# A decoder layer on one core: where the feed-forward weights are prepared, and a norm that is called two up steps later

## The chip, the cores and the metric

The kernel runs on one core of a Trainium2 chip. The metric is the device time of one execution in microseconds (us). The core has a matrix engine (TensorE, PE in the rows; PEld is its weight load), VectorE (DVE), ScalarE (ACT), GpSimd (POOL), and SyncE (SP), whose queue starts the DMA transfers. Each engine works through its own instructions in a fixed order.

## The reference, cut to what matters

One layer of a hybrid decoder over a prompt of 2048 tokens and a sample group of 32 tokens. The change lies at its end:

```
x  = x + concat(ya, yb, yc, yd) @ w_out            # (tokens, 1024)
hn = rmsnorm(x, norm_ffn_g)
x  = x + square(relu(hn @ w_up)) @ w_down          # 1024 -> 4096 -> 1024
y  = rmsnorm(x, norm_final_g)
```

## The kernel before, in words

All matrix products are done with pairs of 16-bit halves: a float32 operand is scaled and split into a high half (a copy on ScalarE) and a low half (a subtraction on VectorE, `split`, L176 and L177), and three products stand for one. The products of the feed-forward stage are also arranged as a fast 2x2 block scheme with seven products instead of eight, so operands are first added and subtracted in blocks (`combine` for the activations, four GpSimd passes for the weights, L2036 to L2039 and L2062 to L2065).

**Blocks and chunks.** The prompt is cut into four blocks of 512 tokens, each two pairs of 128-token tiles. The feed-forward stage holds two blocks at a time: first blocks 2 and 3 (`s` = 0), then 0 and 1 (`s` = 1). Block 2 also carries the sample's tokens: its hn has 136 columns a pair, 272 together, where the others have 256. The 4096 hidden columns are cut into 16 chunks `c` of 256. A step is (s, c, b): `up` makes seven product groups of 12 matmuls (tiles px and pb), squares and splits them into the tile ht; `down` adds 14 groups of three matmuls of 512 columns into x on VectorE (L2191), and for block 2 first the sample's product from the small tile hs (L2128, L2129) into a pd bank, added to accs (L2166). The loop at the end of `ffn` names up of step n+1, then one preparation, then down of step n.

**Preparation.** `ffn_wu` loads 1 MB of w_up into a staging buffer (ws, tag "sw", two buffers), scales and splits it into wu (two buffers). `ffn_wd` does so for w_down into wd and wdT (tag "w", four buffers, at first held by the weights of w_out). In the first pair of blocks the scale is found as well (`wscale`: a square on ScalarE, one small matmul into a pd bank, a power on GpSimd, four small VectorE steps).

**Before the stage.** `outproj` does the w_out products of blocks 0 and 1, then of block 2, then (L1940) of block 3, each product 48 matmuls into a px bank. After block 2's products come `ffn_wu(0, 0)`, block 2's `norm_pair` twice, and `out_sample`, which loads the sample's input x_s, adds its own w_out product and makes its part of hn. `norm_pair` works tile by tile: square (L1959), root (L150, L151), normalised rows xn (L1962), eight transposes (L144) in two PSUM banks, copied to xt (L1967); then tt by subtractions (L1973 to L1976) and the halves of hn (L1980, L1981).

**Buffers.** Tiles with one tag share a ring of buffers. Tag "xn" (two): the norm's xn, x_s, os and every ht. Tag "cat" (two): the inputs of a w_out product, xt and tt of block 3's norm, and the tile fr of every up. Tag "sw" (two): ws, and xt and tt of the other norms. PSUM: px two banks, pb five, pd one. Inside `ffn` the tag "t", which the transposes use, means pd; in `outproj` at that point it means pb.

**Order.** Instructions are named in the order of the program, which is their priority; a list scheduler then fixes each engine's order at build time, taking the ready instruction that was named first.

Of the kernel before, what the change touches and what calls it, by code (L numbers as in the profile page):

```python
# [10 lines left out]
F16 = mybir.dt.float16  # L11
BF = mybir.dt.bfloat16
I32 = mybir.dt.int32
AF = mybir.ActivationFunctionType
OP = mybir.AluOpType
# [8 lines left out]
NS = 32  # L24
# [3 lines left out]
BLOCKS = [(2, 3), (0, 1)]  # L28
# [75 lines left out]
class K:  # L104
# [1772 lines left out]
    def outproj(self, ctx, mix):  # L1877

        nc, A = self.nc, self.A
# [29 lines left out]
        for b in BLOCKS[1]:  # L1909
            for i in range(2):  # L1910
# [4 lines left out]
                hn = rot.tile([128, 7, 4, 2, 128], F16, name="hnr")  # L1915
# [3 lines left out]
        first = [load(2 * BLOCKS[0][0] + i, BLOCKS[0][0], i) for i in range(2)]  # L1919
# [8 lines left out]
        self.accs = self.hp.tile([128, 8, NS], F32, name="accs")  # L1928
        self.wsc = self.hp.tile([128, 2, 4096 // FC, 2], F32, name="wsc")
        self.x2, self.hn = {}, {}  # L1930
        for b in BLOCKS[0]:
            n = 128 + (NS // 4 if b == BLOCKS[0][0] else 0)
            hn = self.hp.tile([128, 2, 7, 4, 2, n], F16, name=f"hn{b}", tag=f"hn{b}")
            prs = first
            if b != BLOCKS[0][0]:
                prs = [load(2 * b + i, b, i) for i in range(2)]

                for i, t, m in ((i, t, m) for m in (0, 2) for i in range(2) for t in range(2)):
                    product(*prs[i], t, m)
            if b == BLOCKS[0][0]:  # L1940
                self.ffn_wu(0, 0)
            for i in range(2):
                self.norm_pair(prs[i][1], gb, hn[:, i, :, :, :, 0:128], b == BLOCKS[0][1])
            if b == BLOCKS[0][0]:
                self.out_sample(hn, g8)
            self.x2[b] = [x2 for _, x2 in prs]
            self.hn[b] = hn

# [121 lines left out]
    def ffn(self):  # L2070
        nc, A, O = self.nc, self.A, self.O
# [2 lines left out]
        nc.sync.dma_start(gf, dram(A["norm_final_g"], 0, [[0, 128], [1, D]]))  # L2074
        accs = self.accs
        NC_ = 4096 // FC
        self.ffn_wd(0, 0)

        def up(s, c, b):

# [40 lines left out]
                nc.scalar.activation(x, x, AF.Square)  # L2121
            hs = None
            if n > 128:
                hs = self.hp.tile([128, 2, 2, 2, 2, 8], F16, name="hs", bufs=2)
                for m in range(2):
                    for t in range(2):
                        x = C[:, ((0, 2), (3, 1))[m][t], :].rearrange("p (i n) -> p i n", i=2)[:, :, 128:]
                        nc.scalar.activation(hs[:, m, 0, t], x, AF.Copy)  # L2128
                        nc.vector.tensor_sub(hs[:, m, 1, t], x, hs[:, m, 0, t])  # L2129


            ht = self.fp.tile([128, 7, 2, N], F16, name="ht", tag="xn", bufs=2)
# [20 lines left out]
        def down(s, c, b, ht, f):  # L2153
            ht, hs = ht
            n = ht.shape[3] // 2
            wd = self.wts[s, c][2]
            if hs is not None:
                p = self.ps("o", [128, 8, 2, NS])
                for m in range(8):
                    for k in range(2):  # L2160

                        x, o = hs[:, k].rearrange("p a t i n -> p (a t i n)"), p[:, m].rearrange("p a n -> p (a n)")
                        self.mm(o, wd[:, k, 0, m * 128:(m + 1) * 128], x, start=m + k == 0, stop=False)
                        self.mm(o[:, 0:NS], wd[:, k, 1, m * 128:(m + 1) * 128], x[:, 0:NS], start=False, stop=k == 1)
                for a in range(2):
                    nc.vector.scalar_tensor_tensor(accs, p[:, :, a, :], f, accs, op0=OP.mult, op1=OP.add)  # L2166
                if c == NC_ - 1:
                    self.ffn_sample_out(gf)
            for i in range(2):
                if (s, c) in PLAIN:  # L2170
                    down_plain(wd, self.x2[b][i], ht[:, :, :, i * n:i * n + 128], f)
                else:
                    down_pair(wd, self.wts[s, c][3], self.x2[b][i], ht[:, :, :, i * n:i * n + 128], f)
                if c == NC_ - 1:
                    for t in range(2):
                        tok = (4 * b + 2 * i + t) * 128
                        self.final(self.x2[b][i][:, t, :], 128, gf, O["y_prompt"][0, tok:tok + 128, :],
                                   (b, i) != (BLOCKS[1][1], 1))
# [39 lines left out]
                    nc.vector.scalar_tensor_tensor(o, p, f, o, op0=OP.mult, op1=OP.add)  # L2218


        steps = [(s, c, b) for s in range(2) for c in range(NC_) for b in BLOCKS[s]]
        first = BLOCKS[0][0]
        ht, f = up(*steps[0]), None
        for n, (s, c, b) in enumerate(steps):
            if b == BLOCKS[s][0]:

                _, iu, _, _, idn = self.wts[s, c]
                f = self.col("ff", bufs=4)
                nc.vector.tensor_scalar(f, iu, self.ish, 1.0 / RS, op0=OP.mult, op1=OP.mult)
                nc.vector.tensor_mul(f, f, f)  # L2230
                nc.vector.tensor_mul(f, f, idn)
            nx = up(*steps[n + 1]) if n + 1 < len(steps) else None
            if (s, c) != (1, NC_ - 1):
                (self.ffn_wu if b == BLOCKS[s][0] else self.ffn_wd)(s + (c + 1) // NC_, (c + 1) % NC_)
            down(s, c, b, ht, f)
            if s == 0 and c == NC_ - 1:
                self.ffn_load(b, BLOCKS[1][BLOCKS[0].index(b)])
            ht = nx
# [66 lines left out]
```

## Time and profile before

| | |
|---|---|
| median of 3 runs | 2594.4 us (2593.81 to 2594.45) |
| profiled execution | 2598.28 us, span 2596.5 us, mean granted TensorE clock 0.972 |
| busy share | TensorE 94%, VectorE 77%, ScalarE 51%, GpSimd 47% |
| chain that ended last | TensorE 51%, VectorE 16%, GpSimd 13%, DMA 6%, ScalarE 6% |

The span runs from the first to the last instruction of the profiled execution. The feed-forward stage begins near 1293 us and takes the rest. In a timeline a row is a start, a length, the engine, the line in the kernel, the operation with output and input, a count, and in brackets how long the engine stood idle before it and what ended that. The length of a row with several instructions runs to the end of the last.

### The profile page before, as it was taken

How to read it: one execution, taken by the hardware profiler on the slowest of the kernel's cores; microseconds unless marked ns; L12 is line 12 of the kernel's file. 1: busy time of each engine (PE TensorE's matmuls, PEld its weight loads, DVE VectorE, ACT ScalarE, POOL GpSimd, SP SyncE). 2: the span in 40 equal slices, each digit the busy share in tenths (PEclk: the TensorE clock that was granted, in tenths of full speed). 3: DMA queues.
4: the chain of work that ended last, by engine and by line, in shares of the span. 5: the costliest groups of instructions: out<-in, count | busy, mean ns of one | idle time of the engine just before them, and what ended most of it. 6: DMA issues, size and time to landing. Idle time of an engine off the chain costs nothing.

```text
span 2596.5 us, 51309 instructions
## 1 busy us (share of the span) xinstructions
PE 2439.7 (94%) x20496; PEld 1663.5 (64%) x20496; DVE 2010.8 (77%) x3746; ACT 1313.2 (51%) x2449; POOL 1212.3 (47%) x1265
## 2 busy tenths in 40 slices
PE   7989999999999899999979999999998999999997
PEld 6975554454467677689856666666665666666664
DVE  7566667874576777654589998889997898999996
ACT  6534332033346677562455555665556454555554
POOL 3403122223114566550255555656556665666652
PEclk9989999999999998999979999999999999999999
DMA  6333416879632433356111111111135211121201
GB/s 176 102 81 86 99 30 218 302 248 334 224 101 77 136 96 104 101 171 216 52 41 50 51 64 50 49 66 34 62 124 214 74 62 49 53 66 49 66 33 65
DMA packets 209321, 277.78 MB, mean 107 GB/s; under 512 B 42837, under 2 KB 177106, under 8 KB 198810
## 3 DMA queue, kind: packets, MB, share of 16 engines
q1 hardware_dynamic: 195050, 202.65, 25.0%
q0 software_dynamic: 9376, 67.64, 7.2%
q10 hardware_dynamic: 4656, 4.23, 0.5%
q8 instruction: 160, 2.62, 0.4%
q14 instruction: 79, 0.65, 0.1%
HBM read 217.33 MB, written 54.29 MB: 105 GB/s over the span
## 4 chain that ended last, share of the span: by engine, by line
PE 51%; DVE 16%; POOL 13%; DMA 6%; ACT 6%; issue 5%; SPq 1%; POOLq 0%; DVEq 0%; ACTq 0%
PE pb L140 25%; PE px L140 23%; DVE x L2191 4%; DVE wu L177 2%; PE pd L140 2%; DMA kp<-in_cache_v_dram,ptV 1%; DVE wd L177 1%; PE pb L144 1%; POOL ht L2146 1%; POOL ws L2037 1%; POOL ht L2148 1%; DVE wdT L177 1%; POOL ws L2039 1%; POOL ws L2038 1%; POOL ws L2036 1%
## 5 line engine op out<-in xcount | busy, mean ns | idle before, releaser
L140 PEld LDWEIGHTS <-wu 128*128 128x128 f16 x5376 | 530.3, 99 | 222.9 <-issue 37.3
L2191 DVE SCALAR_TENSOR_TENSOR x<-pb,ff,x 128x512 f32<-128x512 f32 x840 | 591.3, 740 | 27.3 <-PE pb L140 23.3
L140 PE MATMUL px<-hn,wu 128*128 128x256 f16 (+1 forms) x3072 | 428.0, 276 | 14.6 <-DVE hn L1981 7.0
L140 PEld LDWEIGHTS <-ht 128*128 128x128 f16 x2712 | 264.5, 99 | 231.6 <-issue 26.0
L140 PE MATMUL pb<-wdT,ht 128*128 128x512 f16 x1440 | 379.8, 381 | 15.8 <-DVE x L2191 9.2
L140 PE MATMUL px<-xT,w 128*128 128x512 f16 (+1 forms) x1968 | 371.9, 341 | 1.5 <-ACT da L731 1.2
L140 PE MATMUL pb<-wd,ht 128*128 128x512 f16 x1272 | 336.8, 381 | 6.1 <-DVE x L2191 5.2
L140 PE MATMUL pb<-hn,wu 128*128 128x256 f16 (+1 forms) x2304 | 303.6, 277 | 15.8 <-DVE x L2191 7.6
L140 PEld LDWEIGHTS <-w 128*128 128x128 f16 x2160 | 168.6, 99 | 188.1 <-issue 30.9
L909 POOL TENSOR_TENSOR pl<-P,ph 128x512 f16<-128x512 f32 (+3 forms) x160 | 166.9, 1053 | 155.5 <-ACT ph L906 59.6
L176 ACT ACTIVATE wu<-ws,wsc 128x1024 f16<-128x1024 f32 (+1 forms) x128 | 129.4, 1036 | 130.8 <-POOL ws L2039 76.7
L140 PE MATMUL px<-w,cat 128*128 128x256 f16 x1536 | 180.2, 274 | 3.4 <-DMA cat<-cat 3.3
L177 DVE SCALAR_TENSOR_TENSOR wu<-ws,wsc,wu 128x1024 f16<-128x1024 f32 (+1 forms) x128 | 168.6, 1331 | 18.0 <-ACT wu L176 17.7
L140 PEld LDWEIGHTS <-cat 128*128 128x128 f16 x1536 | 149.6, 98 | 25.7 <-DMA cat<-cat 3.4
L140 PE MATMUL px<-w,xT 128*128 128x128 f16 (+1 forms) x2400 | 156.1, 225 | 10.2 <-DVE v L576 4.5
L140 PEld LDWEIGHTS <-xT 128*128 128x128 f16 (+1 forms) x2672 | 153.1, 101 | 15.5 <-issue 5.5
L902 ACT ACTIVATE P<-pb,nck,cc 128x512 f32<-128x512 f32 (+3 forms) x160 | 112.2, 710 | 75.4 <-PE pb L140 69.7
L2143 ACT ACTIVATE ht<-fr 128x1024 f16<-128x1024 f32 (+1 forms) x60 | 64.2, 1070 | 159.9 <-POOL fr L2149 159.9
L2146 POOL TENSOR_TENSOR ht<-fr,ht 128x512 f16<-128x512 f32 (+1 forms) x60 | 84.2, 1403 | 113.0 <-ACT ht L2145 113.0
L2062 POOL TENSOR_TENSOR ws<-ws 128x512 f32<-128x512 f32 x30 | 41.1, 1371 | 187.1 <-DVE wd L177 187.1
L871 DVE TENSOR_REDUCE mx<-pb 128x1 f32<-128x512 f32 (+3 forms) x160 | 94.8, 607 | 40.0 <-PE pb L140 38.9
L2120 ACT ACTIVATE fr<-fr 128x256 f32<-128x256 f32 (+1 forms) x192 | 77.0, 414 | 90.5 <-DVE fr L2101 89.7
(717 smaller groups left out, 4647.1 us busy)
## 6 DMA issues: line engine op xcount, KB each, us to landing
ws<-in_w_up_dram SPq DMA_DIRECT2D x32, 1024.0 KB
ws<-in_w_down_dram SPq DMA_DIRECT2D x32, 1024.0 KB
ws<-in_w_in_dram SPq DMA_DIRECT2D x22, 512.0 KB
x<-in_x_prompt_dram SPq DMA_DIRECT2D x16, 512.0 KB
cat<-cat SPq DMA_DIRECT2D x32, 256.0 KB
x<-in_x_prompt_dram SPq DMA_DIRECT2D x8, 1024.0 KB
out_y_prompt_dram<-x SPq DMA_DIRECT2D x32, 256.0 KB
hnD<-hnr SPq DMA_DIRECT2D x4, 1792.0 KB
```

Of the source, the lines that this page charges most:

```text
L140: self.nc.tensor.matmul(out, lhsT, rhs, start=start, stop=stop, skip_group_check=True)
L144: self.nc.tensor.transpose(out, in_, self.ident[:n, :n])
L176: self.nc.scalar.activation(hi, x, AF.Copy, scale=sc)
L177: self.nc.vector.scalar_tensor_tensor(lo, x, sc, hi, op0=OP.mult, op1=OP.subtract)
L871: nc.vector.tensor_reduce(mx[:, ii, jb:jb + 1], s[:, :n], axis=AX.X, op=OP.max)
L902: nc.scalar.activation(P[:, :n], s[:, :n], AF.Exp, bias=nck[:, j, h, kt:kt + 1], scale=cc[:, h // 2:h // 2 + 1])
L909: (nc.gpsimd if 1 else nc.vector).tensor_sub(pl[:, :n], P[:, :n], ph[:, :n])
L2062: nc.gpsimd.tensor_sub(B11, B12, B11)
L2120: nc.scalar.activation(x, x, AF.Relu)
L2143: nc.scalar.activation(ht[:, o:o + m, 0, :], x, AF.Copy)
L2146: nc.gpsimd.tensor_sub(ht[:, 0:2, 1, :], C[:, 0:2, :], ht[:, 0:2, 0, :])
L2191: nc.vector.scalar_tensor_tensor(o, p, f, o, op0=OP.mult, op1=OP.add)
```

## The change

`ffn_wu` of chunks 0 and 1 are both named before block 2's norm. `ffn_wd` of chunk 0 is named in the middle of block 3's products. Block 3's norm is kept as two calls in `self.late`, made in the loop of `ffn` after two ups. The steps start with block 2 in chunks 0 and 1, then block 3 in chunks 0 and 1; the later ones alternate as before. After each down one preparation is named: w_down of the next chunk after an even step, w_up of the chunk after that after an odd one. The factor f is kept for each chunk. hs gets another layout and is made by two ScalarE copies and two VectorE subtractions a chunk instead of four each; the sample's matmuls read it with a stride.

```diff
--- before.py
+++ after.py
@@ -1928,6 +1928,8 @@
         self.accs = self.hp.tile([128, 8, NS], F32, name="accs")
         self.wsc = self.hp.tile([128, 2, 4096 // FC, 2], F32, name="wsc")
         self.x2, self.hn = {}, {}
+        self.ffn_wu(0, 0)
+        self.ffn_wu(0, 1)
         for b in BLOCKS[0]:
             n = 128 + (NS // 4 if b == BLOCKS[0][0] else 0)
             hn = self.hp.tile([128, 2, 7, 4, 2, n], F16, name=f"hn{b}", tag=f"hn{b}")
@@ -1936,13 +1938,17 @@
                 prs = [load(2 * b + i, b, i) for i in range(2)]
 
                 for i, t, m in ((i, t, m) for m in (0, 2) for i in range(2) for t in range(2)):
+                    if (i, t, m) == (0, 0, 2):
+                        self.ffn_wd(0, 0)
                     product(*prs[i], t, m)
+            norms = [lambda x=prs[i][1], h=hn[:, i, :, :, :, 0:128], last=b == BLOCKS[0][1]: self.norm_pair(x, gb, h, last)
+                     for i in range(2)]
             if b == BLOCKS[0][0]:
-                self.ffn_wu(0, 0)
-            for i in range(2):
-                self.norm_pair(prs[i][1], gb, hn[:, i, :, :, :, 0:128], b == BLOCKS[0][1])
-            if b == BLOCKS[0][0]:
+                for norm in norms:
+                    norm()
                 self.out_sample(hn, g8)
+            else:
+                self.late = norms
             self.x2[b] = [x2 for _, x2 in prs]
             self.hn[b] = hn
 
@@ -2074,7 +2080,6 @@
         nc.sync.dma_start(gf, dram(A["norm_final_g"], 0, [[0, 128], [1, D]]))
         accs = self.accs
         NC_ = 4096 // FC
-        self.ffn_wd(0, 0)
 
         def up(s, c, b):
 
@@ -2121,12 +2126,13 @@
                 nc.scalar.activation(x, x, AF.Square)
             hs = None
             if n > 128:
-                hs = self.hp.tile([128, 2, 2, 2, 2, 8], F16, name="hs", bufs=2)
-                for m in range(2):
-                    for t in range(2):
-                        x = C[:, ((0, 2), (3, 1))[m][t], :].rearrange("p (i n) -> p i n", i=2)[:, :, 128:]
-                        nc.scalar.activation(hs[:, m, 0, t], x, AF.Copy)
-                        nc.vector.tensor_sub(hs[:, m, 1, t], x, hs[:, m, 0, t])
+
+                hs = self.hp.tile([128, 2, 4, 2, 8], F16, name="hs", bufs=2)
+                for q in range(2):
+                    x = C[:, 2 * q:2 * q + 2, :].rearrange("p o (i n) -> p o i n", i=2)[:, :, :, 128:]
+                    d = [hs[:, a, q:4 - q:3 - 2 * q] for a in range(2)]
+                    nc.scalar.activation(d[0], x, AF.Copy)
+                    nc.vector.tensor_sub(d[1], x, d[0])
 
 
             ht = self.fp.tile([128, 7, 2, N], F16, name="ht", tag="xn", bufs=2)
@@ -2159,9 +2165,9 @@
                 for m in range(8):
                     for k in range(2):
 
-                        x, o = hs[:, k].rearrange("p a t i n -> p (a t i n)"), p[:, m].rearrange("p a n -> p (a n)")
+                        x, o = hs[:, :, 2 * k:2 * k + 2].rearrange("p a t i n -> p a (t i n)"), p[:, m]
                         self.mm(o, wd[:, k, 0, m * 128:(m + 1) * 128], x, start=m + k == 0, stop=False)
-                        self.mm(o[:, 0:NS], wd[:, k, 1, m * 128:(m + 1) * 128], x[:, 0:NS], start=False, stop=k == 1)
+                        self.mm(o[:, 0], wd[:, k, 1, m * 128:(m + 1) * 128], x[:, 0], start=False, stop=k == 1)
                 for a in range(2):
                     nc.vector.scalar_tensor_tensor(accs, p[:, :, a, :], f, accs, op0=OP.mult, op1=OP.add)
                 if c == NC_ - 1:
@@ -2218,21 +2224,28 @@
                     nc.vector.scalar_tensor_tensor(o, p, f, o, op0=OP.mult, op1=OP.add)
 
 
+
         steps = [(s, c, b) for s in range(2) for c in range(NC_) for b in BLOCKS[s]]
-        first = BLOCKS[0][0]
-        ht, f = up(*steps[0]), None
+        steps[1], steps[2] = steps[2], steps[1]
+
+        chunks = [(s, c) for s in range(2) for c in range(NC_)]
+        prep = [p for n in range(1, len(chunks))
+                for p in [(self.ffn_wd, chunks[n])] + [(self.ffn_wu, c) for c in chunks[n + 1:n + 2]]]
+        ht, f = up(*steps[0]), {}
         for n, (s, c, b) in enumerate(steps):
-            if b == BLOCKS[s][0]:
+            if (s, c) not in f:
 
                 _, iu, _, _, idn = self.wts[s, c]
-                f = self.col("ff", bufs=4)
-                nc.vector.tensor_scalar(f, iu, self.ish, 1.0 / RS, op0=OP.mult, op1=OP.mult)
-                nc.vector.tensor_mul(f, f, f)
-                nc.vector.tensor_mul(f, f, idn)
+                f[s, c] = g = self.col("ff", bufs=4)
+                nc.vector.tensor_scalar(g, iu, self.ish, 1.0 / RS, op0=OP.mult, op1=OP.mult)
+                nc.vector.tensor_mul(g, g, g)
+                nc.vector.tensor_mul(g, g, idn)
             nx = up(*steps[n + 1]) if n + 1 < len(steps) else None
-            if (s, c) != (1, NC_ - 1):
-                (self.ffn_wu if b == BLOCKS[s][0] else self.ffn_wd)(s + (c + 1) // NC_, (c + 1) % NC_)
-            down(s, c, b, ht, f)
+            while self.late:
+                self.late.pop(0)()
+            down(s, c, b, ht, f[s, c])
+            if n < len(prep):
+                prep[n][0](*prep[n][1])
             if s == 0 and c == NC_ - 1:
                 self.ffn_load(b, BLOCKS[1][BLOCKS[0].index(b)])
             ht = nx
```

## Rows read from the trace of the kernel before

**Rows 1.** Page, first part: busy us (share of the span) x instructions.

```profile
PE 2439.7 (94%) x20496; PEld 1663.5 (64%) x20496; DVE 2010.8 (77%) x3746; ACT 1313.2 (51%) x2449; POOL 1212.3 (47%) x1265
```

**Rows 2.** Windows: length, busy of PE, PEld, DVE, ACT, POOL, granted clock, DMA.

```profile
1293.00:1333.00 40.00, 22.21 (x137) 17.00 (x136) 35.90 (x37) 25.01 (x34) 23.05 (x16) 0.66 0.13 46
1333.00:1357.00 24.00, 22.35 (x179) 15.51 (x178) 13.54 (x29) 16.18 (x33) 11.18 (x14) 0.93 0.10 35
1357.00:1900.00 543.00, 521.09 (x3868) 348.78 (x3866) 492.84 (x789) 315.09 (x562) 317.72 (x295) 1.00 0.16 53
1900.00:2060.00 160.00, 148.15 (x1032) 98.08 (x1031) 138.43 (x196) 91.52 (x177) 103.98 (x99) 0.96 0.43 153
2060.00:2520.00 460.00, 454.53 (x3106) 304.52 (x3104) 426.88 (x564) 234.72 (x432) 288.62 (x247) 0.99 0.17 56
...
1943.00:1948.00 5.00, 4.88 (x28) 3.57 (x28) 4.32 (x8) 0.80 (x2) 0.00 (x0) 0.55 0.90 330
```

**Rows 3.** Timeline of PE: start us, length us, work [idle before <- releaser].

```profile
1257.62 35.23 PE L140 MATMUL px<-w,cat 128*128 128x256 f16 x319
1292.68 1.91 PE L144 MATMUL pb<-cst,xn 128*128 128x128 f32 x16
...
1294.57 1.55 PE L140 MATMUL px<-hn,wu 128*128 128x272 f16 x12
...
1303.39 1.97 PE L144 MATMUL pb<-cst,xn 128*128 128x128 f32 x8 [4.21 <-DVE wsc L191]
1305.15 4.94 PE L140 MATMUL pb<-hn,wu 128*128 128x272 f16 x24
...
1353.84 2.75 PE L140 MATMUL pb<-wdT,ht 128*128 128x512 f16 x12
...
1943.12 4.91 PE L140 MATMUL pb<-hn,wu 128*128 128x256 f16 x24 [4.45 <-DVE x L2191]
```

**Rows 4.** Timelines of ACT, then DVE: the norm's steps.

```profile
1206.38 0.60 ACT L1967 ACTIVATE xt<-pd 128x512 f32<-128x512 f32 x1 [2.68 <-PE pd L144]
...
1211.75 1.04 ACT L1959 ACTIVATE xn<-x 128x1024 f32<-128x1024 f32 x1
...
1280.11 1.04 ACT L1959 ACTIVATE xn<-x 128x1024 f32<-128x1024 f32 x1
...
1277.34 0.48 DVE L1981 TENSOR_TENSOR hn<-os,hn 128x128 f16<-128x128 f32 x2
...
1282.17 1.28 DVE L1962 SCALAR_TENSOR_TENSOR xn<-x,n_rstd,gb 128x1024 f32<-128x1024 f32 x1 [3.56 <-POOL n_rstd L151]
```

**Rows 5.** Timeline of SP's queue.

```profile
1246.17 0.35 SPq L1987 DMA_DIRECT2D x_s<-in_x_sample_dram  x1
```

**Rows 6.** Timelines of DVE, then POOL: preparation of chunk 0, the sample's chain.

```profile
1241.58 0.15 DVE L191 TENSOR_SCALAR wsc<-w_m 128x1 f32<-128x1 f32 x1
...
1259.05 0.69 DVE L1973 TENSOR_TENSOR tt<-xt 128x512 f32<-128x512 f32 x1
...
1260.52 5.82 POOL L2007 TENSOR_TENSOR os_rs<-os_rs,mhalf 128x32 f32<-128x32 f32 x1 [4.01 <-DVE os_rs L2006]
```

**Rows 7.** Groups: page, then DVE 1330 to 1960, then ACT 1500 to 2500.

```profile
L2062 POOL TENSOR_TENSOR ws<-ws 128x512 f32<-128x512 f32 x30 | 41.1, 1371 | 187.1 <-DVE wd L177 187.1
...
L177 DVE SCALAR_TENSOR_TENSOR wdT<-ws,wsc,wdT 128x2048 f16<-128x2048 f32 x15 | 36.4, 2427 | 6.8 <-ACT wdT L176 6.7
...
L2129 DVE TENSOR_TENSOR hs<-fr,hs 128x16 f16<-128x16 f32 x64 | 33.7, 532 | 10.7 <-ACT hs L2128 10.7
...
L176 ACT ACTIVATE wdT<-ws,wsc 128x2048 f16<-128x2048 f32 x25 | 50.0, 2000 | 9.2 <-POOL ws L2065 8.3 <-PE pb L140 0.3
```

**Rows 8.** Waits 1357 to 1900: total us, times, longest; then tile hs: min/median/max ns.

```profile
PE pb L140 <- DVE x L2191: 15.8, 18, 2.3
PE pb L140 <- ACT fr L2098: 2.8, 3, 1.3
...
L2129 DVE TENSOR_TENSOR hs<-fr,hs x64: 155/496/1261, 1330.8 to 1943.6; 128x16 f16<-128x16 f32 x64
```

## The prediction, as it was put on record

> **What bounds the kernel now.** I read the busy shares first: TensorE is busy 94% of the span and VectorE 77% [rows 1]. Then windows by stage, to see where TensorE is not busy. From 1357 to 1900 us (the feed-forward stage, first pair of blocks) it idles 21.9 of 543 us, from 2060 to 2520 us (second pair) only 5.5 of 460, with VectorE above 90% in both [rows 2]. The gap that this change aims at is 1293 to 1333: TensorE does 137 instructions in 40 us at a mean granted clock of 0.66, while VectorE is busy 35.9 us [rows 2]. Third, TensorE's timeline there: the products of w_out end at 1292.9, then come short groups of transposes and up matmuls with waits between them, one of 4.2 us [rows 3].
>
> The same lines show what I rest most on. The first product group of the first up step (tile px, 12 matmuls) runs at 1294.6, but its next two (tile pb) only at 1305.2, behind the transposes of the other block, which write pb too [rows 3]. Their operands were there: the last piece of the first block's hn was written at 1277.8 [rows 4]. So **a ring of buffers is handed out in program order**: a later tile gets none before every earlier one of that tag has one. A second sign: the sample input x_s, whose load needs nothing but a buffer of tag xn, was issued at 1246.2 [rows 5], though between 1206.4 and 1211.8 both xn buffers were empty [rows 4, 5]; the tiles named before it had to come first.
>
> **The change part by part, with every ring followed.**
>
> *Two chunks staged first.* The w_up slices of chunks 0 and 1 now take both staging buffers (tag sw) before the first block's norm does. Both loads are early: the norm before ends a little after the first block's own square has run (1211.8 [rows 4]). But the norm's xt then has to wait until chunk 0 has been prepared. That preparation gets its scale at 1241.7 and ends with the split at 1259.0; the norm's tt waits for just that today [rows 6]. Now xt gets a buffer at 1255 to 1259, and tt when chunk 1 is done, four GpSimd passes of about 1.4 us later, near 1262. What is late next: the five pb banks fill with transposes, so xn is freed near 1257 instead of 1245 and x_s loads 11 us later. The sample's projections hold one of the two px banks until x_s is added to them, a few us after its load; until about 1263 the products have one bank and wait for VectorE between two of them, twice or so, 1.3 us each: **3 us lost** (0 if the banks turn out free, 6 if VectorE is behind with splits). The sample's chain took 31.6 us from that load to its last hn piece (1246.2 to 1277.8 [rows 4, 5]), so it ends near 1289, before the products (1296).
>
> *w_down of chunk 0 inside the products.* Its work leaves the gap: VectorE 2.4 twice and ScalarE 2.0 twice (one shape), four GpSimd passes of 1.37 [rows 7]. Staged when the norm frees a buffer near 1280, it is ready near 1306 and is needed at 1315. It is hidden under two up steps. If that cover were gone, it would cost what it costs today.
>
> *Two ups, then a down, before the late norm.* A product matmul of 256 columns takes 0.110 us (319 in 35.2 [rows 3]), one of 272 0.117; two ups of 84 make 19.6 us, a down of 42 at 0.22 (12 in 2.75 [rows 3]) 9.2. So TensorE is covered from 1296 to 1325. The late norm, though, can't use that time: its xn comes behind two ht tiles in a ring of two, and the first of these is free only when the first down is over, 1325. The second ht waits for a down which stands behind the late block's own up in the pb ring. So the norm runs with one xn buffer, alone. A tile takes 3.35 us from the square to the normalised rows (1280.1 to 1283.45 [rows 4]), then two batches of transposes and copies through a single pd bank, about 1.45 us each (0.60 is the copy [rows 4]): the next tile starts 5.6 us after the one before. Four tiles, with one GpSimd pass of 1.7 in between, are through at 23.6 us; the differences, the ScalarE copy and VectorE's remainder (the shape of a split of w_down, 2.0 and 2.4 [rows 7]) end at 29.7. The first up matmuls can go at 25.5. **Gap: 25.4 us**, less 3.8 of transposes (16 in 1.91 [rows 3]): 21.6 lost, and the restart adds 2.2: after a wait of 4.5 us, 24 such matmuls took 4.91 us instead of 2.75, at a granted clock of 0.55, mostly the lower of its two levels (1.2 of 2.4 GHz) [rows 2, 3].
>
> *w_down of chunk 1.* Its scale product needs the pd bank, behind those eight batches and the first down's sample product. So it starts at about 1351; the scale (an estimate of 3.7: four VectorE steps of 0.15 [rows 6], a GpSimd power and the waits between), then ScalarE 2.0, VectorE 2.4, GpSimd 5.5, ScalarE 2.0, VectorE 2.4 [rows 7] make 18 us: ready at 1369, with TensorE out of other work at 1366. **3 us lost.** Bounds: 0, and 10 if passes interleave.
>
> *Sum of the start.* Until four ups and four downs are done (some 80 us of TensorE work) the loss now would be 3 + 21.6 + 2.2 + 3 = 30, with the usual 1 to 2 besides. Before: 137 instructions at about 0.115 are 15.8 of 40 us, so 24.2 lost; 1.7 idle and about 1 by clock up to 1357; 2 at the later idle rate [rows 2]: 29. The gap is moved and not closed: **+1**, between -9 (no bank wait, a second xn buffer) and +11.
>
> *Steady steps.* A preparation moves ahead of one up, and stands as before between two downs. Rings sw, pd and the weights keep their order, so each becomes possible at the same moment: 0, with 5 either way for the reshuffled order.
>
> *Sample halves (hs).* Four subtractions a chunk become two: 64 cost 33.7 us at a mean of 532 ns, and VectorE waited 10.7 us for their copies [rows 7]. I take half of each: 17 us of VectorE and 5 of waits in a stage where TensorE lost 15.8 us to late additions [rows 8]. TensorE feels a part; the first pair of blocks idles 4.0% against 1.2% in the second, 15 us more, and hs is about a quarter of the extra VectorE work: **-4**. Bounds 0 and -10. The same instruction takes 155 ns at its shortest, 1261 at its longest [rows 8], while GpSimd passes last about 1.4 us. The Trainium skill (SBUF — State Buffer, Who interferes with whom) says that a VectorE operation with two SBUF inputs and a GpSimd operation that reads SBUF exclude each other, the second waiting out the first. By that the excess over 155 ns isn't the subtraction's own, and if the next two-input operation inherits it, 5 us are saved instead of 17, and the sum changes by -1 instead of -4.
>
> *Pass from the first to the second pair of blocks:* TensorE idles 11.9 us between 1900 and 2060 [rows 2]; the rings there are as before. I put -2, between -6 and +4.
>
> Total -5. The profiled execution took 2598.3 us (span 2596.5, 1.8 around it), 3.9 above the median; 2598.3 - 5 = 2593.3 there, **2589** beside the median of 2594.4.
>
> **Rivals.**
> 1. *The gap closes.* If the late norm gets buffers early, its 30 us lie under two ups and a down (29 us) and only some 6 us of the start's 30 remain: -24, with hs and the pass -30: 2564. For: VectorE is free then. Against: [rows 3, 5].
> 2. *Slower: the sample's chain.* Every matmul of the first up reads the sample's columns. Today the chain holds a 5.8 us GpSimd power [rows 6], and it will stand behind chunk 1's passes and splits. It decides once it ends after 1303: each us past 1296 is a us. 14 us late gives -5 + 14: 2603. For: every step of it is on VectorE or GpSimd, busier than before. Against: 7 us of slack.
> 3. *Slower: preparation before up.* With weights first, ScalarE may serve a 2.0 us split ahead of a 0.4 us copy that the up waits for. 0.3 us in each of 60 steps is 18 us: 2607. Against: TensorE lost only 2.8 us to its costliest such copy from 1357 to 1900 [rows 8].
> 4. *The subtractions' waits are inherited,* and the pass gives nothing: 2594, no change. The steps: 155 ns times 32 saved, -1, and the +1 of the start.
>
> **How the numbers follow.** Forecast 0.45 (own range 2580 to 2597), rival 1 0.17, rival 2 0.12, rival 3 0.10, rival 4 0.16. 0.2% is 5.2 us, about what a measurement of this kernel can tell from no change. The forecast lies at that edge: half of it counts as faster, most of the rest as the same. So faster 0.44 (0.23 + 0.17, and 0.04 from the favourable side of rival 4), same 0.32, slower 0.24. The range 2565 to 2603 leaves out the far half of rival 1, of rival 2 and most of rival 3.
>
> **What would show it.** Right: TensorE busy from the last w_out product to about 1325, then one gap near 25 us with eight batches of transposes into pd; the late norm's first square right behind the last matmul of the first down; 32 hs subtractions; the wdT of chunk 1 after 1360. Wrong: squares of the late block before any down has ended, or more than 5 us idle between the last w_out product and the first up; a steady idle rate other than 3 to 4%.

## The result, and the profile after

The changed kernel takes 2607.8 us in the median, the kernel before 2594.1 us: a ratio of 1.006, with a 95% interval of 1.0044 to 1.0077. It is 14 us slower.

The first line of the page of the kernel after stands beside [rows 1]: TensorE is as busy as before, VectorE 7 us more, although it has 32 instructions less.

```profile
PE 2439.7 (94%) x20496; PEld 1664.0 (64%) x20496; DVE 2017.4 (77%) x3714; ACT 1308.6 (50%) x2417; POOL 1231.1 (47%) x1265
```

Its windows, with the columns of [rows 2]:

```profile
1293.00:1333.00 40.00, 28.84 (x197) 19.52 (x194) 19.22 (x30) 17.52 (x41) 11.97 (x16) 0.89 0.09 27
1333.00:1357.00 24.00, 11.40 (x80) 8.04 (x80) 14.44 (x15) 9.66 (x14) 5.66 (x6) 0.61 0.07 23
1357.00:1900.00 543.00, 510.20 (x3763) 341.49 (x3763) 486.44 (x747) 310.85 (x524) 331.12 (x288) 0.99 0.16 51
1900.00:2060.00 160.00, 147.71 (x1034) 97.20 (x1032) 141.65 (x193) 90.44 (x181) 105.72 (x98) 0.98 0.43 153
2060.00:2520.00 460.00, 459.25 (x3162) 309.00 (x3161) 432.98 (x571) 238.21 (x437) 292.65 (x251) 1.00 0.18 58
```

The hole has moved from the first window to the second. The first pair of blocks (third window) idles 32.8 us where [rows 2] had 21.9; only 1.6 of them belong to the end of the hole, up to 1362.6. The second pair (last window) is as full as before.

Code that the change doesn't touch ran 8.9 us faster in the profiled execution of the kernel after, so I count from a point A, the first matmul of the sample's w_out product (tile catS; 1241.5 us before, 1232.6 after). Milestones in us after A, read from the timelines of TensorE and VectorE: the end of block 3's products, the starts of the sample's additions (tile accs) of chunks 2 and 15, the span's end; the last column, the second pair, is the difference of the two before it. At the addition of chunk 2 both orders of steps have the same downs behind them.

| kernel | products | chunk 2 | chunk 15 | end | second pair |
|---|---|---|---|---|---|
| before | 51.3 | 183 | 713 | 1355.0 | 642 |
| after | 57.8 | 199 | 733 | 1372.7 | 640 |

So +16 at the start, +4 in the rest of the first pair, -2 in the second. That is +18 where the medians differ by 14; the stretch ahead of A differs by several us from execution to execution (A lies between 1231 and 1248 us in the kernels of this study).

TensorE's timeline of the kernel after shows the start: a wait and matmuls at half speed in block 3's products, the last matmuls of the first down, and what follows until work is dense again. Line numbers are each kernel's own: the norm's square, L1959 before, is L1965 here.

```profile
1246.81 5.49 PE L140 MATMUL px<-w,cat 128*128 128x256 f16 x25 [3.28 <-DVE x L1907]
...
1321.96 0.81 PE L140 MATMUL pb<-wd,ht 128*128 128x512 f16 x3 [0.51 <-DVE x L2197]
1326.24 1.12 PE L144 MATMUL pd<-cst,xn 128*128 128x128 f32 x4 [3.46 <-DVE xn L1968]
1328.04 1.12 PE L144 MATMUL pd<-cst,xn 128*128 128x128 f32 x4 [0.69 <-ACT xt L1973]
1333.11 1.11 PE L144 MATMUL pd<-cst,xn 128*128 128x128 f32 x4 [3.95 <-DVE xn L1968]
...
1341.53 1.09 PE L144 MATMUL pd<-cst,xn 128*128 128x128 f32 x4 [5.50 <-DVE xn L1968]
...
1347.08 1.01 PE L140 MATMUL px<-hn,wu 128*128 128x256 f16 x4 [2.67 <-ACT hn L1986]
1348.36 1.12 PE L144 MATMUL pd<-cst,xn 128*128 128x128 f32 x4 [0.27 <-DVE xn L1968]
1349.50 3.37 PE L140 MATMUL px<-hn,wu 128*128 128x256 f16 x20
1352.71 0.60 PE L144 MATMUL pd<-cst,xn 128*128 128x128 f32 x4
...
1359.00 3.08 PE L140 MATMUL pb<-hn,wu 128*128 128x256 f16 x14 [0.64 <-ACT hn L1986]
```

ScalarE's squares of the four tiles, and VectorE's last piece of hn, which the rest of that up needs:

```profile
1322.81 1.06 ACT L1965 ACTIVATE xn<-x 128x1024 f32<-128x1024 f32 x1 [5.30 <-PE pb L140]
...
1329.69 1.05 ACT L1965 ACTIVATE xn<-x 128x1024 f32<-128x1024 f32 x1
...
1336.56 1.05 ACT L1965 ACTIVATE xn<-x 128x1024 f32<-128x1024 f32 x1
...
1344.95 1.05 ACT L1965 ACTIVATE xn<-x 128x1024 f32<-128x1024 f32 x1
...
1358.98 2.29 DVE L1987 TENSOR_TENSOR hn<-tt,hn 128x2048 f16<-128x2048 f32 x1 [0.43 <-ACT hn L1986]
```

The reader is to see three things. The first square starts right where the first down's last matmuls end. The tiles follow each other in 6.9, 6.9 and 8.4 us. And the up resumes in earnest only with the last pieces of hn, at 1359 to 1361, not when its first groups can go at 1347.

### The profile page after: what moved, and what is told of

The parts are those of the page before. It is cut to its first block, busy times and chain, and to the rows that moved or that the text cites. A ratio compares the mean times of both kernels' runs of the same rounds, so it can differ in the third digit from the quotient of the medians.

```text
span 2605.3 us, 51260 instructions
## 1 busy us (share of the span) xinstructions
PE 2439.7 (94%) x20496; PEld 1664.0 (64%) x20496; DVE 2017.4 (77%) x3714; ACT 1308.6 (50%) x2417; POOL 1231.1 (47%) x1265
## 4 chain that ended last, share of the span: by engine, by line
PE 59%; DVE 15%; POOL 11%; ACT 5%; DMA 5%; issue 4%; SPq 1%; POOLq 0%; DVEq 0%; ACTq 0%
PE pb L140 28%; PE px L140 26%; DVE x L2197 3%; PE pd L140 2%; DVE wu L177 1%; DVE wd L177 1%; PE pb L144 1%; POOL ws L2043 1%; PE pd L144 1%; POOL ws L2044 1%; POOL ws L2045 1%; POOL ht L2152 1%; POOL fr L2144 1%; DVE s5cat L480 1%; POOL ws L2042 1%
## 5 line engine op out<-in xcount | busy, mean ns | idle before, releaser
L2197 DVE SCALAR_TENSOR_TENSOR x<-pb,ff,x 128x512 f32<-128x512 f32 x840 | 589.3, 741 | 26.8 <-PE pb L140 25.4
L140 PEld LDWEIGHTS <-w 128*128 128x128 f16 x2160 | 167.5, 99 | 184.8 <-issue 25.4
L177 DVE SCALAR_TENSOR_TENSOR wu<-ws,wsc,wu 128x1024 f16<-128x1024 f32 (+1 forms) x128 | 175.5, 1383 | 21.6 <-ACT wu L176 21.5
```

Source lines behind the costliest of these rows:

```text
L140: self.nc.tensor.matmul(out, lhsT, rhs, start=start, stop=stop, skip_group_check=True)
L177: self.nc.vector.scalar_tensor_tensor(lo, x, sc, hi, op0=OP.mult, op1=OP.subtract)
```

## The experiments

Theory 1 was that the start, with its late norm, is the loss; the rival, that the new place of the preparations costs in every step. A third cause came out of the first four runs. All milestones stand in one table behind the last group; ratios there are to the kernel before on the same chip.

**One part alone, one part undone.** hs_only is the kernel before with the new hs. norm_at_once undoes the late norm:

```diff
+            for norm in norms:             # for both blocks
+                norm()
+            self.late = []
...
-            else:
-                self.late = norms
...
-        steps[1], steps[2] = steps[2], steps[1]
```

wu1_later moves one line. late_own_xn gives the late norm buffers of tag w:

```diff
-        self.ffn_wu(0, 1)                     # wu1_later
+                self.ffn_wu(0, 1)             # behind self.out_sample(hn, g8)
...
-            xn = self.fp.tile([128, D], F32, name="xn", tag="xn", bufs=2)   # late_own_xn
+            xl = xl if t else self.wp.tile([128, 2, D], F32, name="xl", tag="w") if last else None
+            xn = xl[:, t] if last else self.fp.tile([128, D], F32, name="xn", tag="xn", bufs=2)
```

> The kernel before with the new hs alone: two subtractions and two copies a chunk in place of four. Theory 1, subtractions cost what they last: 17 us of VectorE go, TensorE feels -4 (step of the prediction), 2590. Theory 2, their length was waiting that the next instruction inherits: -1 to 0, 2593 to 2594; then the mean of a subtraction rises (532 ns before) and VectorE's other groups grow by what is saved.

> The changed kernel with block 3's norm called right behind its products again, and the steps alternating as before; the early w_up of chunk 1, the w_down of chunk 0 among the products and the order down, then preparation, stay. Theory 1, the late norm is the loss: most of the 17 us of the start come back, the slip of some 6 us from the early staging stays, 2596 to 2599. Theory 2, the order of preparation is the loss: 2604 to 2610, with holes in every stretch of the stage.

> The changed kernel with the w_up preparation of chunk 1 named behind the sample's part instead of ahead of block 2's norm. Theory 1, staging two chunks first makes TensorE wait in block 3's products (6 us measured, 3 predicted): the products end 5 to 6 us earlier, all else stays, 2602. Theory 2, the slip is hidden behind the later gap or the preparation of chunk 1 is late in its turn: 2607 to 2609.

> The changed kernel, with the late norm's normalised rows in buffers of tag w (free once block 3's products are over) instead of the ring that it shares with ht. Theory 1, the ring holds the norm back: its first square runs before 1300, not behind the first down (1322.8), the norm ends under the two ups, the gap of 24 us shrinks to under 5, and 18 to 22 us come back, 2586 to 2590. Theory 2, VectorE and ScalarE are too full with the ups' work, or the single pd bank holds it: the gap keeps 10 us or more, 2597 to 2600.

Both theories missed hs_only (2628.3) and norm_at_once (2636.3) by far. The milestones tell where: up to chunk 15 they are 2 and 6 us ahead of the kernel before, and then lose 38 and 50 us in the second pair of blocks, where hs_only does the same work as the kernel before (hs belongs to the sample, which only block 2 carries) and norm_at_once the same as the kernel after. One window of that stage, in the kernel before:

```profile
2080.00:2480.00 400.00, 395.07 (x2697) 264.59 (x2696) 373.13 (x491) 203.51 (x374) 254.13 (x217) 0.99 0.18 59
```

The same window in hs_only, then its waits there (total us, times, longest):

```profile
2080.00:2480.00 400.00, 370.86 (x2501) 246.61 (x2500) 362.44 (x459) 191.89 (x350) 248.49 (x199) 0.99 0.16 53
```

```profile
PE pb L140 <- DVE x L2192: 12.6, 12, 2.7
PE px L140 <- ACT fr L2098: 9.5, 3, 3.2
PE pb L140 <- ACT fr L2098: 6.9, 4, 2.1
```

The same work in another order. The scheduler fixes each engine's order at build time, and any edit changes all that it decides later. Read from the planned order of TensorE, as runs of matmuls of ups into px or pb (Ux, Ub) and of downs (D), the second pair of the kernels before, after, wu1_later and late_own_xn falls into a pattern that repeats itself for 8 to 11 rounds, 168 up and 84 down matmuls (one chunk of both blocks) a round:

```
Ux2 D6 Ux12 D9 Ux3 D3 Ux3 D3 Ux5 D3 Ux13 D6 Ux12 Ub20 D3 Ub3 D3 Ub13 D3 Ux12 D3 Ux6 D6 Ux4 D3 Ux1
D3 Ux1 D3 Ux7 D6 Ux3 D3 Ux2 D3 Ux3 D3 Ux5 Ub13 D3 Ub3 D3 Ub8 Ux2 D2 Ub7 D3 Ub5 D1
```

hs_only and norm_at_once have no such round. This is "the cycle" of the expectations below. The trace shows its price: by VectorE's additions of downs into x, a chunk of both blocks takes 36.7 us within the rounds of the kernel before, and 41 us on average over nine chunks at the same place in hs_only. Why the scheduler falls into it or not I have not found.

wu1_later went about as its theory 2: the products end 5 us earlier (52.5), chunk 2 only 1 us (198). The late norm's first square comes no earlier, 89.8 us after A against 90.2 in the kernel after, so the gain is lost again under the two ups and the first down, before the gap begins. GpSimd, which now has the w_up passes of chunk 1 right in front of w_down's of chunk 0, is busy 18.9 us from 1290.3 to 1322.6 (10.5 us from 1290.4 in the kernel after); that this is the reason is not shown. In late_own_xn the squares leave the ring of ht:

```profile
1295.82 1.04 ACT L1966 ACTIVATE xl<-x 128x1024 f32<-128x1024 f32 x1
...
1298.94 1.04 ACT L1966 ACTIVATE xl<-x 128x1024 f32<-128x1024 f32 x1
```

All four run before 1300, the first 32 us sooner when counted from A, so the ring did hold them. But from 1317 to 1357 TensorE still idles 14 of 40 us (theory 2): the rest of the norm is named behind the ups, and its transposes, through one pd bank, run from 1313 to 1345 (ScalarE copies the first batch out of the bank at 1322.5, 9 us after it is done). Chunk 2 comes 9 us earlier (190), and that is lost again by chunk 15 (731); the time, 2612.9, lies above the range of either theory.

**Does the order alone decide?** at_once_cycle is norm_at_once with one preparation of 62 in another place; before_no_cycle does the like to the kernel before; hs_cycle does it to hs_only at step 24; at_once_wu1_cycle adds the edit of wu1_later to at_once_cycle.

```diff
+            if n < len(prep) and n == 28:      # at_once_cycle
+                prep[n][0](*prep[n][1])
             down(s, c, b, ht, f[s, c])
-            if n < len(prep):
+            if n < len(prep) and n != 28:
                 prep[n][0](*prep[n][1])
```

> norm_at_once with one preparation of 62 (step 28: w_down of chunk 15) named ahead of its down instead of behind it. The work is the same; the planned order of the second pair now has the repeating cycle. Theory 1 (order alone made norm_at_once slow): first pair as in norm_at_once, some 6 us shorter than in the kernel before, second pair some 48 us shorter than in norm_at_once, 2584 to 2590. Theory 2 (something in the second pair costs whatever the order): over 2620.

> The kernel before with one preparation of 62 (step 28: w_up of chunk 15) named behind its down instead of ahead; the planned order of the second pair loses the cycle. Theory 1 (the order decides): the first pair as before within 5 us, the second 35 to 50 us longer, 2627 to 2645. Theory 2 (no such effect): 2592 to 2598.

> hs_only with one preparation of 62 (step 24: w_up of chunk 13) named behind its down instead of ahead, by which the planned order of the second pair has the cycle. Theory 1 (order alone made hs_only slow, hs itself is worth -1 to -3): the second pair some 38 us shorter than in hs_only, 2588 to 2595 with up to 5 us for the one late preparation. Theory 2 (hs costs by itself): over 2620.

> As at_once_cycle, and the w_up preparation of chunk 1 behind the sample's part, so that TensorE doesn't wait in block 3's products. Theory 1 (the 6 us of slip count when no gap follows the first down): 2578 to 2585. Theory 2 (they are hidden behind the norm's gap, as in wu1_later): 2584 to 2590.

For most of the loss, it does. at_once_cycle took 2578.4 us, 58 less than norm_at_once and less than theory 1 said; before_no_cycle took 2635.5, 44 more than the kernel before, within the range of theory 1. The window of the second pair in at_once_cycle, then in before_no_cycle:

```profile
2080.00:2480.00 400.00, 400.00 (x2754) 269.16 (x2753) 377.94 (x500) 205.85 (x382) 252.58 (x218) 1.00 0.18 59
```

```profile
2080.00:2480.00 400.00, 371.37 (x2495) 246.60 (x2493) 359.84 (x455) 190.01 (x346) 246.05 (x199) 0.98 0.16 53
```

hs_cycle got 29 us of the second pair back (651 instead of 680). Its rounds begin at the same down as those of the kernel before and take as long, 36.7 us a chunk; the other 9 us lie ahead of them, where three chunks around the change of pairs (additions 421 to 504 of the downs) take 151 us instead of 141. With 7 us lost at chunk 15 (718, hs_only 711), probably by the one late preparation, it stays at 2608.4, outside the range of theory 1. at_once_wu1_cycle (2582.5) lies in the range of its theory 1, but is no better than at_once_cycle: the products end 7 us earlier (52.5 against 59.3), the addition of chunk 2 comes 1 us later. at_once_cycle is faster than both kernels of this study: 0.9949 of the time before, 0.9928 to 0.9969.

**The place of the preparations.** prep_after is the kernel before with `down` ahead of the preparation in each step, which keeps the weights one chunk ahead; hs_prep_after has the new hs as well; hs_prep_wd0 also w_down of chunk 0 among block 3's products. no_late_norm is norm_at_once with the edit of wu1_later and one empty slot at chunk 8 (`prep.insert(16, (lambda *a: None, (0, 0)))`), so that from there on it has half a chunk less lead.

```diff
+            down(s, c, b, ht, f)                  # prep_after
             if (s, c) != (1, NC_ - 1):
                 (self.ffn_wu if b == BLOCKS[s][0] else self.ffn_wd)(s + (c + 1) // NC_, (c + 1) % NC_)
-            down(s, c, b, ht, f)
```

> The kernel before with each preparation named behind the down of its step, nothing else. Its planned order for the second pair reaches the cycle for a small part only. Theory 1: the first pair as before within 5 us (the term of the steady steps), the second pair 20 us or more longer, 2612 to 2625. Theory 2 (the order of the second pair doesn't matter): 2590 to 2600.

> The kernel before with the new hs and with each preparation named behind the down of its step instead of ahead; the start as before. The planned order of the second pair has the cycle. Theory 1 (order of the second pair decides; hs is worth -1 to -3, the moved preparation 0, as predicted): 2589 to 2594. Theory 2 (the new hs or the moved preparation costs by itself): over 2605.

> As hs_prep_after, and w_down of chunk 0 named among block 3's products. Theory 1: the work leaves the gap (VectorE 4.8 us, ScalarE 4.0, four GpSimd passes), the first sample add comes 3 to 8 us earlier and that much is kept, 2583 to 2589. Theory 2, the gap is held by the late-ending norm alone: 2589 to 2594, as hs_prep_after.

> The changed kernel without its late norm (block 3's norm right behind its products, steps alternating), with the w_up preparation of chunk 1 behind the sample's part, and with one step left without preparation at chunk 8, by which the planned order of the second pair of blocks comes into the repeating cycle that the kernels before and after have and the run norm_at_once lacked. Theory 1 (the late norm is the loss at the start; the second pair's loss in norm_at_once comes from the planned order alone): the first pair ends 6 to 12 us earlier than in the kernel before, the second takes as long as before, 2580 to 2586. Theory 2 (preparation behind the down costs in the second pair, whatever the order): 30 to 45 us stay lost there, 2615 to 2635.

Theory 1 missed all four, and theory 2 has the size wrong in prep_after and hs_prep_wd0. no_late_norm lands in the range of theory 2, but not where that puts the loss: its second pair is as planned (639). The loss of all four is in the first pair, in prep_after for the larger part. Waits of hs_prep_after from 1357 to 1900:

```profile
PE pb L140 <- ACT wu L176: 32.2, 11, 4.1
PE px L140 <- DVE wu L177: 9.8, 10, 2.1
```

Behind the down with a lead of one chunk, the split w_up comes late to almost every chunk: 609 us from chunk 2 to 15 where the kernel before takes 530. With the lead of two chunks that the change gives (norm_at_once) it takes 528. no_late_norm keeps pace up to chunk 9 (464 us after A, 465 before) and loses 31 us from there to chunk 15, behind its empty slot. In the second pair, where no scale is to be found, the order counts again: 638 to 640 us with the cycle, 682 in prep_after without. w_down of chunk 0 among the products is worth 9 us at chunk 2 (186 against 195).

**Late norm or two chunks first?** swap_at_once is the changed kernel with the norm called at once, the swapped steps kept. swap_at_once_pd sends its transposes to the pd bank; swap_at_once_pd_wu1 adds the edit of wu1_later. at_once_cycle_old_hs is at_once_cycle with the hs of before.

```diff
             for norm in norms:
+                self.bank["t"] = "d" if b == BLOCKS[0][1] else "b"    # swap_at_once_pd
                 norm()
```

> The changed kernel with block 3's norm named right behind its products, while the two chunks for block 2 ahead of block 3 stay. Its planned order of the second pair has the cycle. Theory 1 (the place of the norm is what costs): as at_once_cycle, 2576 to 2586. Theory 2 (taking two chunks of block 2 first costs by itself, by preparations that bunch up): 2595 to 2608.

> As swap_at_once, but block 3's norm transposes into the pd bank instead of the pb banks that the ups use. Theory 1 (rings decide): the ups of block 2 need no bank behind the norm's, run dense while the norm goes on, and the gap at the start closes, 10 to 20 us better than swap_at_once, 2562 to 2575. Theory 2 (one pd bank or VectorE holds the norm until the first down anyway): as swap_at_once or worse, 2576 to 2600.

> As swap_at_once_pd, with the w_up preparation of chunk 1 behind the sample's part. Theory 1 (with the gap closed the slip of 6 us in block 3's products counts): 3 to 6 us better than swap_at_once_pd. Theory 2 (the later preparation of chunk 1 competes with the norm): the same or worse.

> at_once_cycle with the hs of the kernel before (four copies and four subtractions a chunk). Both planned orders have the cycle for as many rounds. Theory 1 (hs is worth -1 to -3 in the first pair): 2579 to 2582 where at_once_cycle took 2578.4. Theory 2, the prediction's term (-4, up to -10): 2582 to 2588.

The window from A to the addition of chunk 2, in the kernel before:

```profile
1241.50:1424.50 183.00, 161.54 (x1434) 123.62 (x1432) 144.10 (x227) 101.90 (x174) 87.58 (x77) 0.92 0.15 50
```

In the kernel after:

```profile
1232.60:1431.60 199.00, 166.92 (x1449) 125.81 (x1448) 141.46 (x220) 99.15 (x162) 86.05 (x78) 0.91 0.12 37
```

And in swap_at_once:

```profile
1243.40:1422.40 179.00, 160.46 (x1450) 123.70 (x1448) 140.11 (x220) 99.55 (x164) 87.83 (x78) 0.96 0.12 40
```

TensorE idles 21.5, 32.1 and 18.5 us there. The place of the norm alone makes 20 us at chunk 2 (199 against 179): 13.5 of idle time, the rest longer busy time at a lower clock. Taking two chunks first costs nothing up to there. In the time 12 us are left (2595.4), at the edge of theory 2's range and not in theory 1's: swap_at_once loses 8 us to at_once_cycle between chunk 2 and chunk 15 and 4 in the second pair. Its rounds begin later (8 of them, 11 in at_once_cycle), which a chunk at 36.7 us inside and some 39 just ahead of them bears out for the larger part; whether taking two chunks first costs something by itself later on is not shown. The pd bank made it worse (184 at chunk 2, 2602.3), w_up later worse still at chunk 2 (189) and the same in time (2601.5). The two hs can't be told apart: 2583.7 (ratio 0.9959 to 0.9989) with the old one against 2578.4 (0.9928 to 0.9969). By the medians theory 2 is met, but the intervals overlap, and the profiled executions have the old one 3 us ahead at the end.

| kernel | median | ratio (interval) | products | chunk 2 | chunk 15 | end | second pair |
|---|---|---|---|---|---|---|---|
| hs_only | 2628.3 | 1.0139 (1.0118-1.0159) | 51.3 | 180 | 711 | 1391.0 | 680 |
| norm_at_once | 2636.3 | 1.0164 (1.0142-1.0187) | 57.8 | 179 | 707 | 1398.6 | 692 |
| wu1_later | 2609.6 | 1.0067 (1.0047-1.0088) | 52.5 | 198 | 731 | 1371.2 | 640 |
| late_own_xn | 2612.9 | 1.0078 (1.0056-1.01) | 57.8 | 190 | 731 | 1373.5 | 643 |
| at_once_cycle | 2578.4 | 0.9949 (0.9928-0.9969) | 59.3 | 179 | 710 | 1347.2 | 637 |
| before_no_cycle | 2635.5 | 1.0156 (1.0134-1.0177) | 51.3 | 183 | 717 | 1392.8 | 676 |
| hs_cycle | 2608.4 | 1.0056 (1.0035-1.0077) | 51.3 | 180 | 718 | 1368.5 | 651 |
| at_once_wu1_cycle | 2582.5 | 0.9969 (0.9954-0.9984) | 52.5 | 180 | 711 | 1348.2 | 637 |
| prep_after | 2730.4 | 1.0531 (1.051-1.0552) | 51.3 | 195 | 813 | 1495.1 | 682 |
| hs_prep_after | 2685.3 | 1.0351 (1.0329-1.0373) | 51.3 | 195 | 804 | 1444.1 | 640 |
| hs_prep_wd0 | 2671.5 | 1.0305 (1.0285-1.0325) | 51.8 | 186 | 795 | 1433.3 | 638 |
| no_late_norm | 2619.3 | 1.0108 (1.009-1.0127) | 52.5 | 182 | 744 | 1383.0 | 639 |
| swap_at_once | 2595.4 | 1.0011 (0.9998-1.0024) | 59.4 | 179 | 718 | 1358.8 | 641 |
| swap_at_once_pd | 2602.3 | 1.0051 (1.0033-1.0069) | 57.8 | 184 | 722 | 1363.3 | 641 |
| swap_at_once_pd_wu1 | 2601.5 | 1.0041 (1.0028-1.0054) | 52.6 | 189 | 725 | 1362.2 | 637 |
| at_once_cycle_old_hs | 2583.7 | 0.9974 (0.9959-0.9989) | 57.8 | 180 | 703 | 1343.9 | 641 |

## Why the prediction was wrong, step by step

**The start: +16 instead of +1.** The picture was right: the ups run dense behind the products, the first square stands behind the first down (1322.81), eight batches go through pd, and the first up matmuls of block 3 come 24.3 us after the down (25.4 forecast). Three windows of the kernel after (columns of [rows 2]) price it; the first is the two ups and the first down, the next two are the gap up to and behind the first up matmuls:

```profile
1290.40:1322.60 32.20, 29.04 (x211) 20.27 (x209) 18.38 (x28) 15.79 (x35) 10.51 (x12) 1.00 0.11 34
1322.77:1347.08 24.31, 6.67 (x25) 4.43 (x25) 11.63 (x11) 12.16 (x18) 5.35 (x9) 0.53 0.00 0
1347.08:1362.60 15.52, 10.92 (x87) 8.00 (x87) 10.31 (x15) 5.30 (x7) 2.32 (x2) 0.74 0.11 35
```

I take TensorE's busy time, times the granted clock, for the work done, and the rest of a window for lost; that is an estimate. Up to the first up matmuls 20.8 us are lost, as forecast (21.6). The step that failed is the end of the gap, "the restart adds 2.2": behind the first up matmuls another 7.4 us are lost. The forecast ended the gap where the up's first groups can go. They are 24 of its 84 matmuls; the groups in pb need the last pieces of hn, at the end of the chain. That chain is also longer: 38.5 us from the first square to the last piece (1358.98 + 2.29) where I had 29.7. I had spaced the tiles by 5.6 us, with a batch of four transposes as in a dense stretch [rows 3]. Here TensorE stands idle between them, the granted clock is 0.5 (the lower of its two levels), and a batch takes 1.12 us, where the one in a dense stretch (1352.71) takes 0.60. And the last batch stands behind 20 up matmuls in TensorE's order (1349.50): it starts 4.35 us after the one before, where the second batch of the first two tiles starts 1.80 us after the first.

Two terms in front of the gap were too small as well. "TensorE is covered from 1296 to 1325" put at nothing what came to 3.2 us. **The slip in the products** was 6.5 us, beyond its upper bound of 6 (forecast 3). With the gap's 4.4 (28.2 against 23.8) these are 11 of the 15 us that the start is off. A part of the rest is order: by the addition of chunk 2 the kernel after has done 15 matmuls more (1449 against 1434). Against the same kernel with the norm at once (swap_at_once) the late norm costs 20 us at chunk 2. The slip isn't won back by moving the preparation of chunk 1 alone: wu1_later gained 1 us.

**w_down of chunk 0** was indeed hidden. The sum has no term of its own for that; between hs_prep_after and hs_prep_wd0 it is worth 9 us at chunk 2. **w_down of chunk 1** was ready at 1375.8 (its last split starts at 1373.4 and takes 2.35), 1369 forecast; TensorE waited 0.9 us for it, not 3.

**Steady steps, 0 with 5 either way:** +4 after, -2 in norm_at_once. But a sign of being wrong that the prediction named is there: an idle rate of 3 to 4% was expected, and TensorE idles 31.2 of 537.4 us (5.8%) from 1362.6 to 1900. The term holds only with the change's second chunk of lead; I had not named that lead as the cover. With one chunk, the same move costs 87 us between chunk 2 and chunk 15 (prep_after), 79 with the new hs.

**Sample halves, -4:** open. Up to chunk 15 hs_only is 2 us ahead of the kernel before, at_once_cycle is 7 us behind at_once_cycle_old_hs, and the medians of that pair differ by 5 us the other way. VectorE's list from 1357 to 1900 shows what became of its own time; the kernel before, then hs_only, both with 14 chunks of subtractions:

```profile
L177 DVE SCALAR_TENSOR_TENSOR wu<-ws,wsc,wu 128x1024 f16<-128x1024 f32 (+1 forms) x52 | 65.7, 1276 | 5.2 <-ACT wu L176 5.0
...
L2129 DVE TENSOR_TENSOR hs<-fr,hs 128x16 f16<-128x16 f32 x56 | 29.5, 534 | 6.8 <-ACT hs L2128 6.8
```

```profile
L177 DVE SCALAR_TENSOR_TENSOR wu<-ws,wsc,wu 128x1024 f16<-128x1024 f32 (+1 forms) x52 | 67.8, 1315 | 9.4 <-ACT wu L176 9.1
...
L2130 DVE TENSOR_TENSOR hs<-fr,hs 128x32 f16<-128x32 f32 x28 | 18.3, 655 | 3.0 <-ACT hs L2129 3.0
```

hs gives back 11.2 us, but each subtraction left is 121 ns longer, and 52 splits of w_up take 2.1 us more. So a part is inherited; that all of it beyond 155 ns is, as rival 4 had it, isn't shown. The Trainium skill (SBUF — State Buffer, Who interferes with whom) says that a VectorE operation with two SBUF inputs contends with a GpSimd operation that reads SBUF; the longer mean (655 against 534 ns) agrees with it, though the order and the shape changed as well (the shortest takes 176 ns in the kernel after, 155 before). In the kernel after the same 52 splits take 72.1 us, but that is not the work of hs. The splits of at_once_cycle, then of at_once_cycle_old_hs, with the new and the old hs, are about equally long:

```profile
L177 DVE SCALAR_TENSOR_TENSOR wu<-ws,wsc,wu 128x1024 f16<-128x1024 f32 (+1 forms) x53 | 77.3, 1468 | 10.3 <-ACT wu L176 9.5
```

```profile
L177 DVE SCALAR_TENSOR_TENSOR wu<-ws,wsc,wu 128x1024 f16<-128x1024 f32 (+1 forms) x54 | 78.1, 1458 | 5.6 <-ACT wu L176 5.0
```

**The pass, -2, and the second pair:** it came out at -2, by luck. "The rings there are as before" is not what decides. Builds with the cycle take 637 to 643 us there (651 in hs_cycle), those without 676 to 692. A swing of some 40 us stood in no term, rival or bound.

**Rivals.** Rival 3 named the right time (2607) by a wrong road: TensorE's waits for fr from 1357 to 1900 are 4.2 us. Rival 2 did not occur: the first up starts right behind the products (1290.31). Rival 1, the closed gap, stays unreached: late_own_xn and swap_at_once_pd each free one ring, and the gap stays. In late_own_xn the single bank, copied out late (1322.5), holds the norm; in swap_at_once_pd TensorE waits 5.3 and 6.0 us (up to 1307.34 and 1318.02) for copies on ScalarE. Rival 4's inheritance is seen in part in hs_only.

## What to carry to other kernels

Where a list scheduler fixes the order at build time, a neutral edit can be worth more than the edit under study: compare the planned orders first, and time a variant that moves one harmless instruction before you believe a single part. Count by stages from a common point, so that a loss in a stage that the edit doesn't touch gives itself away. Price a deferred chain to its last piece, at the speed that its engines have when they stand idle between steps; and when a preparation is named behind its consumer's step, ask what lead hides it.

## What the hardware showed that I had not expected

hs_only and the kernel before have the same instructions up to A, in the same order, and reached it 7.8 us apart (1233.7 and 1241.5 us): a difference of that size between two single spans says nothing. Counted from A, executions agree better. The kernel before and before_no_cycle, one program up to step 28, stay within 0.5 us of each other over 650 us; norm_at_once and at_once_cycle stay within 2 us.

Batches of four transposes that follow idle time took 1.09 to 1.12 us, at a granted clock of 0.5, against 0.60 in a dense stretch (1352.71 above).
